# A hybrid decoder layer on one core: the first gated head's products stand two products further behind its loads, and the fourth raw block of the values is loaded later

## The chip, the core and the metric

The kernel runs on one core of one Trainium2 chip. The core has TensorE for matrix products (PE; its weight loads are listed apart as PEld), VectorE (DVE), ScalarE (ACT), GpSimd (POOL) and SyncE (SP), whose queue issues most of the transfers between the chip's memory and the core. Each engine runs its own instructions in order; semaphores order them among each other. The metric is the device time of one execution in microseconds (us). A measurement gives the median of several runs.

## The reference

One layer with 1024 tokens of width 1024, in float32. After an RMS norm, one in-projection gives nine groups of columns; eight heads of differential softmax attention and four heads of gated linear attention (GLA) work on them side by side; the out-projection joins both.

```python
h = rms_norm(x, pre_g)
z = jnp.einsum('bsd,de->bse', h, w_in)            # w_in: 1024 x 7184
qa, ka, va, ga, qb, kb, vb, gb, gk_low = split_columns(z)
oa = diff_attention(qa, ka, va, lam)              # 8 heads, values 128 wide
oa = rms_norm(oa, subln_g) * (1.0 - lam_init) * silu(ga)
log_a = log_sigmoid(gk_low @ w_gk_up + b_gk) / 16
ob = gla_chunked(qb, kb, vb, log_a)               # 4 heads, keys 128, values 256 wide
ob = rms_norm(ob, gla_g) * silu(gb)
return x + rms_norm(concatenate([oa, ob]) @ w_out, post_g)
```

(Shapes and reshapes are left out.) In `gla_chunked` a state of 128 x 256 per head is carried from chunk to chunk; within a chunk the decayed queries and keys give a masked score matrix that multiplies the values.

## The kernel before

**The in-projection** is done as products of 2 x 2 blocks with seven block products in place of eight. The columns of `w_in` are taken in 26 pairs p; the pair's weights fall into four raw blocks b11, b21 (left columns, top and bottom rows) and b12, b22 (right columns). Seven products n = 1, 2, 5, 6, 4, 7, 3 multiply one block, or one sum of blocks, with a block of the normed input. (p, n) names a product. Float32 accuracy is had by splitting each operand into a high part (ACT casts it) and a low part (DVE subtracts), so a product is three rounds of four matmuls of 128 x 512, 12 in all. Products land in accumulator banks called x (n = 1, later 6 and 7 on top), y (n = 2 or 4) and z (n = 5, later 3); `take_bank` hands out the eight banks from a list, the longest free first.

The list `order` holds the 182 products. The values of the attention heads are pairs 22 and 23 (`VALS`), done together with weights twice as wide, so that one of their products is 24 matmuls into two banks. Around them `order` runs (21,7), (22,1), (21,3), (23,1), (22,2), (23,2), (22,5), (23,5), (22,6), (23,6), (22,7) and so on through n = 4 and 3. Then pairs 24 and 25 follow.

`go(n)` emits the next n products. For each it first prepares the weights of this and the next three products (`prepare`, `make_weights`; L333 subtracts raw blocks, L352 makes high parts, L353 low parts). The weights lie in a ring of `NRING` = 5 tiles. For the values `value_weights` does this: `load_values` loads a raw block in two halves (L214), L302 subtracts blocks in place, L306 makes the two high tiles and L309 the two low ones, so that a value product's weights take four of the ring's five places. Its blocks b11 and b21 have buffers of their own. The two halves of b12 take the buffers tagged `q0` and `k0`, those of b22 `k1` and `q1`, which the gated heads use before: a load waits until the old reader is through. The third part of `go` advances a side stream, `fill`: once per product, and twice per value product.

```python
va, vb = VALS
order += [(va, 1), (va - 1, 3), (vb, 1)] + [(p, n) for n in (2, 5, 6, 7, 4, 3) for p in VALS]
...
    go(order.index((9, 3)) + 1 - made[0])
    fill.append(chain(*(gla(g) for g in range(GLA_HEADS))))
    go(len(order) - made[0] - LEAD)
```

**The gated heads** are that side stream. It begins when product (9,3) is emitted, so its first step stands behind (10,2). `gla(g)` is a generator that runs two halves of 512 tokens; between two `yield`s stand the steps of a half: the loads of keys and queries `kq` (L847, L848), values `gv` (L850) and decayed queries `gqd` (L851); the score products `pa` and the transposes `pk` (L117, L120), masked on POOL (L872), and the loads of the gates (L881); the state products `kv`; the output products `gpo` (po in the text); the squares, and the loads for the next half; the norm's product `gms`, the norm and gating on DVE (L944 to L950) and four stores to `mixe` (L952). Only the first half's loads stand directly ahead of their use; every later half's loads are issued four steps ahead. `kq` has the buffer `q0`, `gv` `k0`, `gqd` `q1`, and `k1` holds the masked scores, later the squares `sq_hl` that `gms` multiplies.

After a value product, `take_heads` adds the sums on DVE (L462), which frees the y bank, splits them (L463, L464) and stores them (L466). The weights of the out-projection are split on the side too (`wo_step`, L667 to L687, through POOL's queue).

The matmuls keep the order of the program (`keep_in_program_order`). On the other engines and on SP the order is chosen at build time by a scheduler that simulates the timeline; what stands later in the program may go earlier there.

When the 182 products end, the attention scores, values and the out-projection follow, again with an order of matmuls that is fixed at build time.

Of the kernel before, what the change touches and what calls it, by code (L numbers as in the profile page):

```python
# [31 lines left out]
def hymba_kernel(  # L32
# [23 lines left out]
    def fp(t):  # L56
        return t.bitcast(F32)
# [127 lines left out]
    def load_raw(p, halves=(0, 1)):  # L185
        if p >= len(pairs):
            return
        if p in VALS:
            return load_values("b11")
        c0 = pairs[p][2]  # L190
        for kh in halves:
            if kh not in raws.setdefault(p, {}):
                r = ap.tile([P, HB, 256], F32, tag="raw", name="w_raw", bufs=4)
                rows = slice(kh * 512, kh * 512 + 512)
                sp.dma_start(r, w_in[0, rows, c0 : c0 + 256].rearrange("(k p) c -> p k c", p=P))
                raws[p][kh] = r
# [5 lines left out]
    def load_values(name):  # L202

        if name not in value_raws:
            c0 = VA + (name[2] == "2") * 512
            r0 = (name[1] == "2") * 512
            value_raws[name] = []
            for i, tag in enumerate({"b12": ("q0", "k0"), "b22": ("k1", "q1")}.get(name, ("raw",) * 2)):
                if tag == "raw":
                    r = ap.tile([P, 2, 512], F32, tag=tag, name="v_raw", bufs=4)  # L210
                else:
                    r = kp.tile([P, 2, 512], F32, tag=tag, name="v_raw")
                rows = slice(r0 + i * 256, r0 + i * 256 + 256)
                sp.dma_start(r, w_in[0, rows, c0 : c0 + 512].rearrange("(k p) c -> p k c", p=P))  # L214
                value_raws[name].append(r)
# [74 lines left out]

    def value_weights(n):

        for name in {1: ("b11", "b21"), 2: ("b12",), 5: ("b22",), 3: ()}.get(n, ()):
            load_values(name)
        if n in (7, 4):
            load_raw(y if n == 7 else z)
        b11, b12, b21, b22 = (value_raws.get(name) for name in ("b11", "b12", "b21", "b22"))
        src = {1: b11, 2: b21, 5: b11, 6: b11, 7: b12, 4: b21, 3: b22}[n]
        sums = {5: ((b11, b12),), 6: ((b11, b22), (b21, b21)), 7: ((b12, b22),)}.get(n, ())
        for dst, a in sums:  # L300
            for i in range(2):
                dve.tensor_tensor(dst[i], a[i], (b12 if n == 7 else b11)[i], ALU.subtract)  # L302
        his, los = [], []
        for i in range(2):
            his.append(ap.tile([P, 2, 512], F32R, tag="ring", name="w", bufs=NRING))
            act.copy(his[i], src[i])  # L306
        for i in range(2):
            los.append(ap.tile([P, 2, 512], F32R, tag="ring", name="w", bufs=NRING))
            dve.tensor_tensor(los[i], src[i], fp(his[i]), ALU.subtract)  # L309
        return his, los  # L310

    def make_weights(i):
# [4 lines left out]
        if p in VALS:  # L317
            ws[i] = ws_wide[p, n] = value_weights(n)
            return
# [535 lines left out]
    def gla(g):  # L855

        u = None
        for half in range(2):
            cs = cols(half)
            kq, v, qd = gla_loads(g, half)  # L860
            gates = kp.tile([P, 2, 512], F32, tag="ks1", name="gg")
            yield
            o = kp.tile([P, 2, 512], F32, tag="ks0", name="go")
            an = kp.tile([P, 2, 4, P], F32, tag="k1", name="gan")
            a, kn = an[:, 0], an[:, 1]
# [20 lines left out]
            for m in range(2):  # L886
                kv, ib = take_bank([P, 2, 256], "kv")
                n = half * 4 + 2 * m
# [91 lines left out]
# [4 lines that stand above are left out]
    for _ in fill[0] if fill else ():  # L984
# [637 lines left out]
```

## Time and profile before

| what | value |
|---|---|
| time, median of 3 runs | 977.96 us (975.04 to 978.9) |
| the profiled execution's own time | 978.01 us |
| its span, first to last instruction | 976.3 us |
| mean granted TensorE clock | 0.997 |
| busy: PE, DVE, ACT, POOL | 953.5, 734.4, 602.5, 193.8 us |
| in-projection's products with the gated stream | about 231 to 549 us |

Times in the profile's rows count from the start of the span. A row of the timeline gives the start, the duration, the engine, the source line, the operation, what it writes and reads, how many in a row, and in brackets how long the engine had been idle before and what released it. All matmuls come from one helper line, L117, and are told apart by the names of their tiles. A matmul's duration is longer than its share of the stream, since matmuls overlap; distances between starts show the pace. A row of waits names who waited for whom, the total, the number of times and the longest. A granted clock of 1.00 is full speed.

### The profile page before, as it was taken

The numbers are of one execution on the slowest core, as the hardware profiler recorded it, in microseconds if no ns is written. First come the engines' busy times: TensorE is split into PE (matmuls) and PEld (weight loads), VectorE is DVE, ScalarE is ACT, GpSimd is POOL, SyncE is SP. The second block draws the span as 40 slices with busy tenths as digits, with TensorE's granted clock in tenths as the row PEclk, the third lists the DMA queues.
The fourth block names the chain that finished last, engine by engine and source line by source line (L and its number), as shares of the span: only waits on it lengthen the run. The fifth ranks groups of instructions, "written<-read, shape, count | busy, mean of one in ns | idle before, by whom it ended". The sixth has DMA issues, their size and how long they took to land.

```text
span 976.3 us, 15029 instructions
## 1 busy us (share of the span) xinstructions
PE 953.5 (98%) x4946; PEld 811.4 (83%) x4946; DVE 734.4 (75%) x1462; ACT 602.5 (62%) x1164; POOL 193.8 (20%) x263
## 2 busy tenths in 40 slices
PE   6999999999999999999999999999999999999997
PEld 5998988887888888888888888878888888888785
DVE  6986598896677778677675667487888888898554
ACT  8642454754677456467675444366776687887773
POOL 4300001212111111121200002121322222443322
PEclk9999999999999999999999999999999999999999
DMA  9442456578576979986763589997656669995777
GB/s 351 146 119 87 135 170 224 175 247 277 186 233 211 317 230 301 296 271 220 250 194 126 163 244 284 396 300 235 212 171 234 230 200 358 342 283 106 151 204 151
DMA packets 152301, 220.39 MB, mean 226 GB/s; under 512 B 16752, under 2 KB 87408, under 8 KB 152128
## 3 DMA queue, kind: packets, MB, share of 16 engines
q1 hardware_dynamic: 138128, 178.80, 56.9%
q0 software_dynamic: 14096, 40.64, 14.3%
q8 instruction: 39, 0.64, 0.3%
q14 instruction: 38, 0.31, 0.1%
HBM read 133.93 MB, written 88.60 MB: 228 GB/s over the span
## 4 chain that ended last, share of the span: by engine, by line
PE 86%; issue 4%; DMA 3%; DVE 3%; ACT 1%; POOL 1%; SPq 0%; DVEq 0%; POOLq 0%; ACTq 0%
PE x L117 21%; PE ypart L117 13%; PE y L117 13%; PE z L117 12%; PE sc L117 7%; PE po L117 5%; PE yps L117 4%; PE wtr L120 3%; PE gpo L117 3%; DMA wo_raw<-in_w_out_dram 1%; PE kv L117 1%; PE pa L117 1%; PE gkl_ps L117 1%; DMA kq<-gq_d 1%; DMA k_d<-qk_st 1%
## 5 line engine op out<-in xcount | busy, mean ns | idle before, releaser
L352 ACT CAST w<-w_raw 128x512 fp32r<-128x512 f32 (+1 forms) x150 | 98.1, 655 | 98.1 <-PE y L117 46.9
L353 DVE TENSOR_TENSOR w<-w_raw,w 128x512 fp32r<-128x512 f32 (+1 forms) x150 | 109.6, 733 | 45.4 <-ACT w L352 45.0
L1145 ACT ACTIVATE p<-p,stt 128x896 f32<-128x896 f32 (+7 forms) x128 | 99.3, 777 | 36.9 <-DVE stt L1135 33.8
L510 ACT COPY s<-x 128x512 f32<-128x512 f32 x72 | 42.2, 586 | 76.9 <-PE x L117 76.4
L677 POOL DMA_DIRECT2D wo_d<-wo_hi x32 | 17.7, 552 | 344.2 <-ACT wo_hi L667 344.2
L1151 POOL TENSOR_SCALAR p<-p,stt,lam 128x1024 f32<-128x1024 f32 (+3 forms) x64 | 56.2, 878 | 147.0 <-DVE stt L1150 141.4
L1135 DVE CUSTOM_DVE_ANT_0 p<-sc,maskt 128x512 f32<-128x512 f32 (+3 forms) x128 | 74.3, 585 | 14.6 <-PE sc L117 13.3
L117 PE MATMUL x<-s_hi,w 128*128 128x512 f32 x320 | 81.3, 397 | 0.0
L117 PE MATMUL z<-s_hi,w 128*128 128x512 f32 x320 | 80.1, 392 | 0.0
L117 PE MATMUL y<-h_hi,w 128*128 128x512 f32 x320 | 80.0, 392 | 0.0
L117 PE MATMUL ypart<-wo_hi,m_hi 128*128 128x512 f32 x192 | 79.5, 414 | 0.1
L117 PE MATMUL ypart<-wo_hi,m_lo 128*128 128x512 f32 x192 | 75.5, 393 | 0.0
L117 PE MATMUL ypart<-wo_lo,m_hi 128*128 128x512 f32 x192 | 75.4, 393 | 0.0
L333 DVE TENSOR_TENSOR w_raw<-w_raw 128x512 f32<-128x512 f32 (+1 forms) x88 | 65.7, 747 | 11.0 <-DMA w_raw<-in_w_in_dram 9.9
L117 PEld LDWEIGHTS x<-s_hi,w 128*128 128x128 f32 x320 | 60.7, 191 | 12.5
L117 PE MATMUL sc<-k,q 128*128 128x512 f32 (+1 forms) x192 | 69.1, 363 | 1.4 <-DVE stt L1135 1.4
L117 PEld LDWEIGHTS y<-h_hi,w 128*128 128x128 f32 x320 | 59.7, 188 | 12.2
L117 PEld LDWEIGHTS z<-s_hi,w 128*128 128x128 f32 x320 | 59.6, 188 | 12.2
L117 PE MATMUL sc<-ks,q 128*128 128x512 f32 (+1 forms) x192 | 66.2, 347 | 0.0
L1193 ACT CAST wt_hi<-wtr 128x512 fp32r<-128x512 f32 (+1 forms) x80 | 42.8, 535 | 25.6 <-PE wtr L120 24.8
L1194 DVE TENSOR_TENSOR wt_lo<-wtr,wt_hi 128x512 fp32r<-128x512 f32 (+1 forms) x80 | 50.6, 633 | 9.5 <-ACT wt_hi L1193 8.8
L1154 DVE SCALAR_TENSOR_TENSOR p<-p,stt,p 128x1024 f32<-128x1024 f32 (+3 forms) x64 | 52.1, 814 | 4.0 <-POOL p L1151 3.8
(236 smaller groups left out, 2311.2 us busy)
## 6 DMA issues: line engine op xcount, KB each, us to landing
w_raw<-in_w_in_dram SPq DMA_DIRECT2D x48, 512.0 KB, 4.7
wo_d<-wo_hi POOLq DMA_DIRECT2D x32, 256.0 KB, 2.9
q<-q_d SPq DMA_DIRECT2D x32, 256.0 KB, 4.9
k<-k_d SPq DMA_DIRECT2D x32, 256.0 KB, 5.4
ks<-k_d SPq DMA_DIRECT2D x64, 128.0 KB, 6.0
v<-v_d SPq DMA_DIRECT2D x16, 512.0 KB, 7.1
wo_raw<-in_w_out_dram POOLq DMA_DIRECT2D x31, 256.0 KB, 4.6
wo_d<-gqd POOLq DMA_DIRECT2D x22, 256.0 KB, 4.0
```

The costliest lines, as they stand in the source:

```text
L117: tc.keep_in_program_order(pe.matmul(*a, **k))
L120: tc.keep_in_program_order(pe.transpose(dst, src, ident))
L333: dve.tensor_tensor(dst, a, b, ALU.subtract)
L352: act.copy(w[0], src)
L353: dve.tensor_tensor(w[1], src, fp(w[0]), ALU.subtract)
L510: act.copy(b[k], ps)
L1135: ins = dve.tensor_tensor_reduce(p[:, a:e], sc[:, : e - a], maskt[:, NZ + P - (e - a) :] if last else maskt[:, : e - a], 1.0, 3e38 if i == ...
L1145: act.activation(p[:, :n], p[:, :n], AF.Exp, bias=st[:, m : m + 1], scale=-1.0, accum_out=st[:, 2 + m : 3 + m],)
L1151: pool.tensor_scalar(p1[:, :n], p1[:, :n], st[:, 5:6], lam, ALU.mult, ALU.mult)
L1154: dve.scalar_tensor_tensor(p0[:, :n], p0[:, :n], st[:, 4:5], p1[:, :n], ALU.mult, ALU.subtract)
L1193: act.copy(hi[:, :n], pt[:, :n])
L1194: dve.tensor_tensor(lo[:, :n], pt[:, :n], fp(hi[:, :n]), ALU.subtract)
```

## The change

Two edits. In `gla`, the first half of the first head yields twice more between its loads and its score products, so that two more products of the in-projection stand between them; every later step of the stream moves back by two turns of `go`. In `value_weights`, the load of the block b22 moves from product n = 5 to n = 6, the first that uses it.

```diff
     def value_weights(n):
-        for name in {1: ("b11", "b21"), 2: ("b12",), 5: ("b22",), 3: ()}.get(n, ()):
+        for name in {1: ("b11", "b21"), 2: ("b12",), 6: ("b22",)}.get(n, ()):
             load_values(name)
...
     def gla(g):
...
             kq, v, qd = gla_loads(g, half)
             gates = kp.tile([P, 2, 512], F32, tag="ks1", name="gg")
             yield
+            if not g and not half:
+                yield
+                yield
             o = kp.tile([P, 2, 512], F32, tag="ks0", name="go")
```

## The prediction

> **What bounds the kernel now.** I read the head of the page first, then busy time by stretches, then what TensorE waited for.
>
> ```profile
> span 976.3 us, 15029 instructions
> 0.00:241.00 241.00, 226.85 (x1329) 199.69 (x1329) 196.49 (x327) 132.47 (x222) 43.12 (x71) 1.00 0.58 191
> 241.00:616.00 375.00, 375.00 (x1815) 316.34 (x1814) 262.13 (x404) 218.79 (x382) 50.42 (x82) 1.00 0.74 238
> 616.00:930.00 314.00, 311.96 (x1633) 262.91 (x1632) 250.99 (x664) 225.90 (x486) 89.68 (x98) 1.00 0.78 244
> 930.00:976.30 46.30, 39.69 (x175) 32.48 (x174) 24.76 (x68) 25.37 (x75) 10.54 (x12) 0.97 0.75 181
> PE xT L120 <- DVE x L565: 9.0, 4, 7.5
> PE pa L117 <- DMA kq<-gq_d: 2.4, 1, 2.4
> PE sc L117 <- DVE stt L1135: 1.4, 3, 1.0
> ```
>
> In a stretch's row stand its length, then the busy time of PE, PEld, DVE, ACT and POOL, the granted clock, the DMA share and GB/s. From 241 to 616 us PE is busy 375.00 of 375.00 us, and from 616 to 930 it lacks 2.04. So almost any microsecond that the in-projection wins or loses is handed on to the end. PE's order is the program's. The one long wait outside the start-up is the one the change addresses: pa, the first product of gated head 0, waits for its loads.
>
> The place itself, PE alone, and the same product seven halves later, where its load is long there:
>
> ```profile
> 235.69 1.07 PE L117 MATMUL z<-s_lo,w 128*128 128x512 f32 x4
> 239.19 1.19 PE L117 MATMUL pa<-kq 128*128 128x128 f32 x8 [2.42 <-DMA kq<-gq_d]
> 240.88 3.31 PE L117 MATMUL x<-s_hi,w 128*128 128x512 f32 x8
> 244.94 1.98 PE L117 MATMUL y<-h_hi,w 128*128 128x512 f32 x8
> ...
> 494.78 1.98 PE L117 MATMUL z<-s_hi,w 128*128 128x512 f32 x8
> 496.60 1.07 PE L117 MATMUL z<-s_lo,w 128*128 128x512 f32 x4
> 497.50 1.05 PE L117 MATMUL pa<-kq 128*128 128x128 f32 x8
> 498.75 2.10 PE L117 MATMUL x<-s_hi,w 128*128 128x512 f32 x8
> 501.60 1.98 PE L117 MATMUL y<-h_hi,w 128*128 128x512 f32 x8
> ```
>
> From the last z group to the next product's y group takes 244.94 - 235.69 = 9.25 us at the wait and 501.60 - 496.60 = 5.00 without one: 4.25 us are lost, not 2.42. Until pa starts it is 3.50 against 0.90, so 2.60; from pa on it is 5.75 against 4.10, so 1.65 more. The clock says why:
>
> ```profile
> 236.80:239.20 2.40, 0.01 (x1) 0.04 (x1) 0.75 (x2) 1.37 (x3) 0.49 (x1) 1.00 1.04 361
> 239.20:241.00 1.80, 1.80 (x13) 1.80 (x13) 1.75 (x3) 1.50 (x3) 1.13 (x3) 0.76 1.07 414
> 241.00:242.00 1.00, 1.00 (x5) 0.81 (x4) 0.00 (x0) 0.59 (x2) 0.64 (x1) 0.50 0.92 356
> 243.00:244.00 1.00, 1.00 (x4) 0.77 (x4) 0.00 (x0) 0.00 (x0) 0.00 (x0) 0.73 0.86 262
> ```
>
> The granted clock falls to 0.50 after the gap and is back at 1.00 by 244. This wait is paid twice, and I take 4.25. The Trainium skill, "TensorE: Matmul & The Clock Gate", section "Part 1: The HAM clock gate (the "warmup" mystery)", lets the clock fall only after an idle window of about 3.4 us. By that a gap of 2.6 us would keep full speed; the trace does not agree, with 0.50 at 241 to 242 us. What the rule would make of the time here is the second rival.
>
> **The two added yields.** They put products (10,6) and (10,4), 2.72 us each (497.50 - 494.78, from the z product's first group to pa), between (10,5) and pa. Is pa then free of waiting, and are the two ready to run?
>
> ```profile
> 231.98 7.07 DMA kq<-gq_d
> 231.42 0.62 ACT L352 CAST w<-w_raw 128x512 fp32r<-128x512 f32 x1 [0.96 <-PE z L117]
> 234.12 0.62 ACT L352 CAST w<-w_raw 128x512 fp32r<-128x512 f32 x1 [2.09 <-PE y L117]
> ```
>
> The later load lands at 231.98 + 7.07 = 239.05. Without the wait (10,6) starts at 235.69 + 0.90 = 236.59 and pa 5.44 later, at 242.03: 3.0 us of margin, and nothing in the change delays that load. The weights ring has five places, so the cast that waited at 234.12 for y of (10,2) belongs to the product five further on, (11,1)'s, and the one at 231.42 is (10,7)'s; (10,6) and (10,4) had theirs before. The wait goes whole: **-4.25 us**. Should the margin fail, 4.25 is the most that stays.
>
> Every later step of the gated stream also runs two products later: in each of eight halves the gate loads (2), the next half's loads (5) and the stores to mixe (4), all on SP, one affine select on POOL, and the ACT and DVE work between. Loads, pa, kv, po and norm keep their spacing in products, PE waits for none of the later halves today, and what they read (keys, queries, values) is stored before the stream begins. I cost these moves at nothing, covered by the in-projection products between the steps; the uncovered price is the 4.25 above. No instruction is added.
>
> **The end of the stream.** The value products (22 and 23) run two stream steps each, so here the shift is not plain. Working the yields through: now po stands behind (22,1) and the norm's product gms behind (22,2); after, po stands behind (23,1) and gms behind (23,2), with (22,5) next. Three things hang on that.
>
> ```profile
> 517.34 0.90 SPq L214 DMA_DIRECT2D v_raw<-in_w_in_dram  x2
> 517.28 2.07 PE L117 MATMUL z<-s_hi,w 128*128 128x512 f32 x8
> 525.54 1.98 PE L117 MATMUL y<-w,h_hi 128*128 128x512 f32 x8
> 521.21 1.23 DVE L302 TENSOR_TENSOR v_raw<-v_raw 128x1024 f32<-128x1024 f32 x1 [7.49 <-DMA v_raw<-in_w_in_dram]
> 534.57 1.05 ACT L306 CAST w<-v_raw 128x1024 fp32r<-128x1024 f32 x1 [0.68 <-PE y L117]
> ```
>
> First, the third raw block, b12, which the diff doesn't name: its second half takes the buffer that po reads, and waits for po to end (517.28, issue 517.34, landed 521.2). Po now ends (21,3) and (23,1) later, 525.54 - 517.28 = 8.26 us, so it lands at 529.5; its subtraction is done by 530.7. The cast that needs it comes at 534.57, when a ring place is free: 3.9 us of slack. Nothing.
>
> ```profile
> 530.98 0.62 PE L117 MATMUL gms<-sq_hl,ones 128*128 128x512 f32 x2
> 531.44 2.16 PE L117 MATMUL y<-w,h_hi 128*128 128x512 f32 x8
> 535.27 1.98 PE L117 MATMUL y<-w,h_hi 128*128 128x512 f32 x8
> 537.09 1.98 PE L117 MATMUL z<-w,s_hi 128*128 128x512 f32 x8
> 547.97 1.98 PE L117 MATMUL x<-w,s_hi 128*128 128x512 f32 x8
> 531.75 0.37 SPq L214 DMA_DIRECT2D v_raw<-in_w_in_dram  x1
> 535.66 1.23 DVE L302 TENSOR_TENSOR v_raw<-v_raw 128x1024 f32<-128x1024 f32 x1 [0.17 <-DMA v_raw<-in_w_in_dram]
> 543.92 0.36 SPq L952 DMA_DIRECT2D mixe<-go  x1
> ```
>
> Second, the fourth raw block, b22: one half takes the buffer that gms reads (issued 531.75, 0.77 after gms starts, landed 3.9 later). Its first user, the weights of (22,6), must be ready at (22,6)'s start. In the new order gms starts 0.46 (531.44 - 530.98) ahead of (22,5), and (22,6) is 547.97 - 537.09 = 10.88 behind that: 11.3 us in all. Needed are 0.77 + 3.9 + 1.23 (subtraction, L302) + 1.05 (cast, L306) = 6.95. Slack 4.4. Behind the load on SP stand only stores, and behind the subtraction on DVE the low halves and the norm's tail. Nothing, while SP issues it when gms ends.
>
> Third, the accumulator banks. While both value halves hold their x sums, four banks circulate. Today's takes are y y, gms, y y, z z, so (23,2)'s second sum takes the bank of (22,2)'s first, which DVE must have read: a wait of 5.65 (537.09 - 531.44) less two products of 2.72, 0.21 us. After, the takes are y y, y y, gms, z z: that 0.21 goes, and (22,5)'s second sum takes the bank of (23,2)'s first.
>
> ```profile
> 540.28 1.28 DVE L462 TENSOR_TENSOR c<-y,s 128x512 f32<-128x512 f32 x2
> 537.40 1.22 DVE L309 TENSOR_TENSOR w<-v_raw,w 128x1024 fp32r<-128x1024 f32 x1
> ```
>
> That matmul, with all of PE's order behind it, would start 0.46 (gms) + 0.23 (one matmul: 537.09 - 535.27 is eight) = 0.69 behind (23,2)'s end. DVE has two low halves (L309, 1.22 each) to make from about 1.8 before that end, when the second group of eight is through: until +0.65; then the read L462 (half of 1.28): until +1.3. A wait of about 0.65. If DVE takes the read first it is 0; if it comes as late as today's (540.28, 3.19 behind that product's end) it is 3.19 + 0.64 - 0.69 = 3.1, and with a halved clock behind it 1.65 more: 4.8. I take 0.65, as DVE loses the norm's tail from just this place.
>
> **Sum**, against the profiled execution's own 978.01 us (span 976.3, 1.7 around it; the three runs' median is 977.96): 978.01 - 4.25 - 0.21 + 0.65 = **974.2**.
>
> **Rivals.** (1) The bank wait is long: value weights are taken ahead of the read on DVE. For it: today's read came 3.19 late. Against: what delayed it was in part the norm's tail. 978.01 - 4.25 - 0.21 + 4.8 = 978.4, no change. (2) The clock's dip at 241 belongs to something else and stays: only 2.60 comes back, 978.01 - 2.60 - 0.21 + 0.65 = 975.9. Against: the clock is 1.00 right up to the gap, falls directly behind it, and the stretches up to 930 us average 1.00. The Trainium skill's idle window of about 3.4 us ("TensorE: Matmul & The Clock Gate", section "Part 1: The HAM clock gate (the "warmup" mystery)") would have it so. (3) Slower: the later load of b22 is put behind the norm's four stores on SP, which wait for DVE. The last of them today is issued at 543.92, 12.94 behind gms. Then the weights of (22,6) are ready at 12.94 + 0.36 + 3.9 + 1.23 + 1.05 = 19.5 instead of by 11.3: a wait of 8.2, and 1.65 for the clock, 974.2 + 9.8 = 984.0. It costs from the point at which the load is issued over 5.2 us behind gms. Against: SP today issues it ahead of those stores. (4) That the change doesn't do what it says (pa still waits) has little for it with 3.0 us of margin, and is counted with (1), as it ends at no change.
>
> **How the numbers follow.** Forecast 0.70, its own range 972.5 to 976.5; rival 1 with 4, 0.12; rival 2, 0.05; rival 3, 0.13. What a measurement here can tell from no change is about 0.5%, 4.9 us: below 973.07 is faster, over 982.85 slower. The forecast is 1.1 us from the first bound, the runs before differ by 975.04 to 978.9, and with no new bank wait it is 973.5; of its 0.70 I give 0.25 to faster. Rivals 1 and 2 are the same, rival 3 is slower: 0.25, 0.62, 0.13. Range 972.0 to 981.0, leaving out the bottom of the forecast and most of rival 3, whose milder forms begin below 981.
>
> **What would show it.** Right: no wait at the first pa, three unbroken products ahead of it, granted clock 1.00 there, the whole stream to the values some 4.3 us earlier; a wait of under 1 us at the z of (22,5) for L462; none at the x of (22,6). Wrong: pa still waiting for kq, a clock dip elsewhere, PE waiting for weights from v_raw at (22,6), or L462 over 2 us behind its product. A PE gap in a stretch where there is none now would say that the shifted ACT and DVE work of the other halves isn't covered.

## The result and the profile after

Over 19 runs of each, the median is 975.10 us after the change (974.23 to 975.85) and 977.66 before (975.04 to 981.25): a ratio of 0.9977, 95% interval 0.9968 to 0.9986. The medians lie 2.6 us apart, and the ratio, which is not the quotient of the medians, gives 2.2 us. The interval leaves out 1, and the gain is under the 0.5% that the prediction called faster. The spread of the runs went from 6.2 us to 1.6.

The page's head, the middle stretch of the busy times and PE's waits of the changed kernel, in the columns of before (its profiled execution took 975.12 us):

```profile
span 973.4 us, 15020 instructions
241.00:616.00 375.00, 373.87 (x1820) 315.62 (x1819) 264.11 (x407) 220.58 (x384) 62.90 (x84) 1.00 0.77 242
PE xT L120 <- DVE x L565: 9.0, 4, 7.6
PE z L117 <- DVE c L462: 1.1, 1, 1.1
```

The line of pa is gone. A new one stands in the list, the z that waits for L462, and the stretch from 241 to 616, full before, now lacks 1.13 us. PE at the first place, with one row of the clock:

```profile
236.13 1.07 PE L117 MATMUL z<-s_lo,w 128*128 128x512 f32 x4
237.04 1.98 PE L117 MATMUL x<-s_hi,w 128*128 128x512 f32 x8
242.48 1.05 PE L117 MATMUL pa<-kq 128*128 128x128 f32 x8
243.72 2.10 PE L117 MATMUL x<-s_hi,w 128*128 128x512 f32 x8
246.57 1.98 PE L117 MATMUL x<-h_hi,w 128*128 128x512 f32 x8
...
241.00:242.00 1.00, 1.00 (x6) 0.83 (x5) 1.00 (x2) 1.00 (x3) 0.60 (x2) 1.00 1.04 410
```

The z of (10,5) is followed at 0.91 by (10,6), pa comes 5.44 later, and from pa to the product after the next it is 246.57 - 242.48 = 4.09, the undisturbed 4.10. The granted clock is 1.00. All 4.25 us came back here.

The second place, PE, DVE and SP from the start of (22,2) to the x of (22,6):

```profile
521.63 2.07 PE L117 MATMUL y<-w,h_hi 128*128 128x512 f32 x8
530.38 1.29 DVE L464 TENSOR_TENSOR c<-c,v_hi 128x512 fp32r<-128x512 f32 x2
531.59 2.35 DVE L309 TENSOR_TENSOR w<-v_raw,w 128x1024 fp32r<-128x1024 f32 x2
532.61 0.62 PE L117 MATMUL gms<-sq_hl,ones 128*128 128x512 f32 x2
533.07 0.40 PE L117 MATMUL z<-w,s_hi 128*128 128x512 f32 x1
533.30 0.37 SPq L214 DMA_DIRECT2D v_raw<-in_w_in_dram  x1
533.87 1.28 DVE L462 TENSOR_TENSOR c<-y,s 128x512 f32<-128x512 f32 x2
534.60 1.89 PE L117 MATMUL z<-w,s_hi 128*128 128x512 f32 x7 [1.14 <-DVE c L462]
545.41 1.98 PE L117 MATMUL x<-w,s_hi 128*128 128x512 f32 x8
```

One matmul of z runs, into the free bank; the second, into the bank of (23,2)'s first sum, starts at 534.60 instead of 533.30. From the first z to the x of (22,6) it is 545.41 - 533.07 = 12.34 against 10.88 before: 1.46 us given back. The load of b22 is issued at 533.30, 0.69 behind gms's start, and the x of (22,6) follows without a wait.

From the z of (10,5) to the y of (22,2) the changed kernel takes 521.63 - 236.13 = 285.50 us and the kernel before 525.54 - 235.69 = 289.85: the 4.35 us that the prediction looked for as "some 4.3". Its other sign, a wait of under 1 us at the z of (22,5), was missed: the list has 1.1, and 1.46 are lost.

In the trace's own terms: 978.01 - 4.25 - 0.21 + 1.46 = 975.01, and the profiled execution took 975.12. That it fits this closely is in part luck: the z of (10,5) comes 0.44 us later than in the profile of before (236.13 and 235.69), and the stretch from the x of (22,6) to the end is 0.3 shorter (973.4 - 545.41 = 428.0 and 976.3 - 547.97 = 428.3).

### The profile page after: what moved, and what is told of

Same layout as the page of the kernel before. It is cut to its first block, busy times and chain, and to the rows that moved or that the text cites. A ratio compares the mean times of both kernels' runs of the same rounds, so it can differ in the third digit from the quotient of the medians.

```text
span 973.4 us, 15020 instructions
## 1 busy us (share of the span) xinstructions
PE 952.3 (98%) x4946; PEld 811.1 (83%) x4946; DVE 734.2 (75%) x1462; ACT 603.0 (62%) x1164; POOL 205.7 (21%) x263
## 4 chain that ended last, share of the span: by engine, by line
PE 93%; DVE 3%; ACT 1%; DMA 1%; issue 1%; POOL 0%; DVEq 0%; SPq 0%; ACTq 0%
PE x L117 24%; PE z L117 15%; PE y L117 14%; PE ypart L117 13%; PE sc L117 7%; PE po L117 5%; PE yps L117 4%; PE wtr L120 3%; PE gpo L117 3%; PE kv L117 1%; PE gkl_ps L117 1%; PE pa L117 1%; DMA v_raw<-in_w_in_dram 1%; PE xT L120 0%; ACT junk L574 0%
```

## The experiments

Each kernel ran beside the kernel before on the same chip; that had a median of 977.15 us beside the first four below (to the filled gap) and of 977.67 beside the others. The ratios are those on record with their intervals, and not the quotients of these medians.

**Only the score products move** (an edit of the kernel before):

```diff
             yield
+            if not g and not half:
+                yield
+                yield
...
             yield
-            yield
-            yield
+            if g or half:
+                yield
+                yield
             us = [u]
```

> Edit of the kernel before: the two yields are added ahead of the first half's score products and two of the three yields behind them are taken away, so that only pa, pk and the gate loads move by two products and the rest of the gated stream, the end at the values and the load of b22 stay as they were. Theory (the wait at pa with its halved clock is worth 4.25 us, and 1.46 us of that is given back at the z of (22,5) in the changed kernel): 4.25 us under the kernel before, about 973.4 us, ratio 0.9957; no wait over 0.3 us at the first pa, clock 1.00 there, and only the old 0.2 us at the y of (23,2). Rival (pa's wait is worth only the 2.6 us that the changed kernel shows): about 975.1 us, ratio 0.9974.

Measured: 974.25 us, ratio 0.9961 (0.9946 to 0.9976). The trace has no wait at pa and none at the z:

```profile
236.55 1.07 PE L117 MATMUL z<-s_lo,w 128*128 128x512 f32 x4
242.90 1.05 PE L117 MATMUL pa<-kq 128*128 128x128 f32 x8
528.05 2.15 PE L117 MATMUL y<-w,h_hi 128*128 128x512 f32 x8
533.67 1.98 PE L117 MATMUL z<-w,s_hi 128*128 128x512 f32 x8
544.55 1.98 PE L117 MATMUL x<-w,s_hi 128*128 128x512 f32 x8
```

From z to x it is 10.88 again; the y of (23,2) keeps its wait (5.62 for 5.44). In time it lies between the two expectations, and its interval holds both; the rows decide for the theory. The first part alone gives the whole gain, and the shift of the stream's end gives some back. The profiled execution took 974.28. What keeps it from 973.4 is in part the start: PE reaches the z of (10,5) at 236.55 here and at 235.69 in the profile of before. Where that spread of the start comes from was not followed.

**The second sum of (22,5) later** (an edit of the changed kernel, in `multiply_values`):

```diff
+        terms = [
+            (j, a, b, k, u)
+            for j, (a, b) in enumerate(((0, hi), (0, lo), (1, hi)))
+            for k in range(HB) for u in range(2)
+        ]
+        if (p, n) == (VALS[0], 5):
+            terms.sort(key=lambda t: t[4])
+        for j, a, b, k, u in terms:
...
```

> Edit of the changed kernel: in product (22,5) all twelve matmuls of the first sum run ahead of the twelve of the second, so that the second sum's bank is wanted 2.7 us later. Theory (the bank wait costs 1.46 us): 1.46 us under the changed kernel and 4.4 us under the kernel before, about 973.4 us, ratio 0.9955; PE has no wait at that z. Rival (those 1.46 us only show up in another wait, the low halves of the weights or a later bank): about 975.1 us, ratio 0.9974.

Measured: 973.85 us, ratio 0.9960 (0.9945 to 0.9976). PE alone:

```profile
532.33 1.09 PE L117 MATMUL z<-w,s_hi 128*128 128x512 f32 x4
534.17 1.98 PE L117 MATMUL z<-w,s_hi 128*128 128x512 f32 x8
543.23 1.98 PE L117 MATMUL x<-w,s_hi 128*128 128x512 f32 x8
```

543.23 - 532.33 = 10.90: the wait is gone and didn't come up elsewhere before (22,6). The median is 1.25 us under the changed kernel's, though measured on other runs and with intervals that overlap. This profiled execution itself gained nothing: it took 975.20 us, the slowest of the five (the others 973.47 to 974.11) and no less than the changed kernel's 975.12. PE reached the x of (22,6) 2.18 us earlier than there and lost that again in the attention, where its list of waits has two lines that the changed kernel's lacks, and a third wait for `stt` of 0.42 us at 814.63:

```profile
PE sc L117 <- DVE wt_lo L1202: 0.5, 1, 0.5
PE sc L117 <- DMA ks<-k_d: 0.5, 1, 0.5
```

So in this execution the rival holds, at a place that it didn't name; the four faster ones have no trace. The medians of this and of the first experiment are the lowest seen, and the two can't be told apart by time.

**Only the load of b22 moves** (an edit of the kernel before; the first part of the diff alone):

> Edit of the kernel before: only the load of b22 moves from n = 5 to n = 6, no yield is added. Theory (its first half waits for gms in any case, and its second is wanted only at n = 6): ratio 1.000 within 0.001, first half still issued right behind gms. Rival (the later load comes too late, or takes DVE or SP time from something else): 1 to 5 us slower, with a wait at the x of (22,6).

Measured: 977.74 us, ratio 1.0008 (0.9995 to 1.0021): no effect, as the theory has it. SP issues the half that waits for gms 0.77 behind gms's start:

```profile
533.20 0.62 PE L117 MATMUL gms<-sq_hl,ones 128*128 128x512 f32 x2
533.97 0.37 SPq L214 DMA_DIRECT2D v_raw<-in_w_in_dram  x1
```

The move gains nothing by itself. By the code, the load's buffers would otherwise be claimed ahead of shifted steps that still use one of them (`sq_hl`), so it goes with the yields; the yields without it weren't tried.

**The gap filled** (an edit of the kernel before):

```diff
+            if not g and not half:
+                idle, ib = take_bank([P, 512], "idle")
+                for _ in range(11):
+                    mm(idle, ones, at(H["h11"][0], 0), start=True, stop=True)
+                free.insert(0, ib)
             pa, ib = take_bank([P, 4, P], "pa")
```

> Edit of the kernel before: eleven matmuls of 128 x 512 whose result nobody reads (11 x 0.227 = 2.5 us) stand ahead of the first pa, in the place of PE's idle time; pa still waits for its loads. Theory (idle PE lets the clock fall, which costs 1.65 us on top of the 2.60): clock 1.00 from 236 to 245 us and 1.65 us less, about 976.0 us, ratio 0.9983. Rival (the dip of the clock has another cause, or the clock falls for a shorter gap too): clock again 0.5 at 241 us and no gain, ratio 1.000.

Measured: 977.51 us, ratio 0.9999 (0.9989 to 1.0009). By time the rival wins, and the trace doesn't decide:

```profile
236.17 1.07 PE L117 MATMUL z<-s_lo,w 128*128 128x512 f32 x4
237.07 2.69 PE L117 MATMUL idle<-h_hi,ones 128*128 128x512 f32 x11
239.82 1.16 PE L117 MATMUL pa<-kq 128*128 128x128 f32 x8
244.03 1.98 PE L117 MATMUL y<-h_hi,w 128*128 128x512 f32 x8
...
241.00:242.00 1.00, 1.00 (x8) 0.85 (x7) 0.00 (x0) 0.99 (x2) 0.33 (x1) 1.00 1.11 408
```

The clock is 1.00, and from z to y it is 7.86 us instead of 9.25. But the loads came early in this execution: the second one of kq was issued at 232.05 and landed 6.7 us later, at 238.75. Without the eleven matmuls the gap would have been about 1.8 us, which is less than one that left the clock at 1.00 (1.96 us, below). So the trace doesn't show that filling a gap keeps the clock. It shows the price: the eleven matmuls cost their 2.5 us also where the loads come sooner, and the expectation had reckoned as if each run of the kernel before lost what its profiled one lost. That asked for its other runs. The expectation's 976.0 was missed by 1.5 us.

**The kernel before again**, two more executions with their traces:

> The kernel before, unchanged, for the spread of its runs. Theory (its runs differ because the wait at the first pa differs, by when the loads are issued, and with it the length of the halved clock): the time goes up and down with the lost time between the z of (10,5) and the y of (10,4): 978.0 us with 4.25 us lost, 975 to 976 with 1 to 2, 980 with 6. Rival (the spread comes from other places): a time that differs by over 1.5 us from this line.

> The kernel before, unchanged, a second time: the same line between the time and the loss at the first pa as in the run before this one.

Measured: 978.34 and 975.71 us. PE in the first and in the second:

```profile
235.83 1.07 PE L117 MATMUL z<-s_lo,w 128*128 128x512 f32 x4
239.50 1.13 PE L117 MATMUL pa<-kq 128*128 128x128 f32 x8 [2.60 <-DMA kq<-gq_d]
245.24 1.98 PE L117 MATMUL y<-h_hi,w 128*128 128x512 f32 x8
```

```profile
235.57 1.07 PE L117 MATMUL z<-s_lo,w 128*128 128x512 f32 x4
238.43 1.13 PE L117 MATMUL pa<-kq 128*128 128x128 f32 x8 [1.79 <-DMA kq<-gq_d]
242.59 1.98 PE L117 MATMUL y<-h_hi,w 128*128 128x512 f32 x8
```

The kernel with only b22's load moved has the same code at this place and makes a fourth case:

```profile
235.81 1.07 PE L117 MATMUL z<-s_lo,w 128*128 128x512 f32 x4
240.14 2.05 PE L117 MATMUL pa<-kq 128*128 128x128 f32 x8 [3.26 <-DMA kq<-gq_d]
247.16 1.98 PE L117 MATMUL y<-h_hi,w 128*128 128x512 f32 x8
```

The gap is pa's start less 0.90 behind the last z group; lost is z to y less the undisturbed 5.00:

| execution | gap, us | lost, us | time, us | time less lost |
|---|---|---|---|---|
| before, second of the two | 1.96 | 2.02 | 975.71 | 973.69 |
| before, profile of the prediction | 2.60 | 4.25 | 978.01 | 973.76 |
| before, first of the two | 2.77 | 4.41 | 978.34 | 973.93 |
| b22's load alone | 3.43 | 6.35 | 980.18 | 973.83 |

The last column is the same within 0.24 us while the time moves by 4.5. So these four executions differ at this one place, and as far as they show, the spread of the kernel before is the spread of this wait. The remainder is not the same for every version: the profiled executions of the score products alone and of one product (below), with nothing lost here, took 974.28 and 975.01. The median of before, 977.66, fits a loss of 3.9; its fastest run, 974.82 beside the first four kernels, one of about 1.

What moves the gap is when the load is issued, not how long it takes. SP issued the second load of kq at 231.31, 231.98, 232.45 and 232.84, in the order of the table, and pa started 7.0 to 7.3 us behind each. In the three longer gaps the profile's chain to pa goes back to a load of the out-projection's weights; in the profile of before it is

```profile
223.25 5.55 DMA wo_raw<-in_w_out_dram
```

When it has landed, ACT and DVE split it (L667, L676); behind that on DVE stand the keys (`c`, L445), and behind their store SP issues the loads. The weights landed at 228.80, 229.28 and 229.68, and the second load of kq was issued 3.2 us later each time. In the shortest gap the chain holds no such load. No run changed this order.

**One product in place of two** (an edit of the kernel before: one added yield, and b22 at n = 6):

> Edit of the kernel before: one added yield in place of two, and b22 loaded at n = 6, so that the first pa stands behind (10,6) and the stream's end moves by one turn: gms stays behind (22,2), po goes behind (21,3). Theory (what is lost at pa is the lateness of the loads, some 0 to 1 us at that place, and the end has only the old bank wait of 0.2 us at the y of (23,2)): a wait of under 1 us at pa with the clock at 1.00, no wait at the z of (22,5); 1 us under the changed kernel, about 974.2 us, ratio 0.997. Rival (a short wait drops the clock as well, or po waits for the state update that now has one product instead of two to run in): 975.5 us or more, with the clock under 1.00 at 241 us or a wait at gpo.

Measured: 974.35 us, ratio 0.9976 (0.9963 to 0.9988). In its profiled execution pa starts at 240.08, unbroken behind (10,6), and the value products have no new wait:

```profile
239.17 1.07 PE L117 MATMUL x<-s_lo,w 128*128 128x512 f32 x4
240.08 1.05 PE L117 MATMUL pa<-kq 128*128 128x128 f32 x8
```

One of its nine runs took 978.04, which none of the other versions without a gap did, and it has no trace. With the start and the loads as in the last case of the table pa would wait here again, but only from 235.81 + 0.90 + 2.72 = 239.43 to 240.14, 0.7 us; where that run lost its 3.7 us isn't known. With the first experiment it shows that the cover may be had without the shift that costs the bank wait.

**Half the gap filled** (five matmuls in place of eleven):

> Edit of the kernel before: five matmuls that nobody reads ahead of the first pa instead of eleven, so that PE idles for 1.4 us in place of 2.5 where the loads land as in the profile of before. Theory (the clock falls once PE has been idle for about two microseconds): clock stays 1.00, time like that with eleven or below, 976.3 us, as the five are less likely to outlast the wait. Rival (any gap over one microsecond drops the clock): clock 0.5 behind the gap and about 977.5 us.

Measured: 975.78 us, ratio 0.9982 (0.9971 to 0.9992).

```profile
237.06 1.31 PE L117 MATMUL idle<-h_hi,ones 128*128 128x512 f32 x5
239.46 1.13 PE L117 MATMUL pa<-kq 128*128 128x128 f32 x8 [1.09 <-DMA kq<-gq_d]
243.62 1.98 PE L117 MATMUL y<-h_hi,w 128*128 128x512 f32 x8
```

From pa to y it is 4.16, so the clock stays up behind an idle time of 239.46 - 237.06 - 5 x 0.227 = 1.27 us. That is against the rival, a drop behind any gap over 1 us. Five matmuls that nobody reads made the kernel faster by 1.8 us (0.0018 x 977.67). That they do so by keeping the clock fits, but isn't shown: without them this gap would have been 239.46 - 237.06 = 2.40 us, between 1.96, which left the clock at 1.00, and 2.60, which halved it.

## Why the prediction was right, point by point

**The wait at pa, -4.25.** It was right in mechanism and size for that execution: the wait and the halved clock went whole, and pa at 242.48 waited for nothing. The margin held, though the second load of kq was issued at 232.99, 1.0 us later than in the profile of before; it landed by 239.9, 2.6 us ahead of pa, where 3.0 had been worked out. The sum was made against one execution whose loss lay near the median, 4.25 against 3.9; had the profile caught the second execution above, the same working would have given 2.02. That the profiled one lay near the median was luck.

**The moved steps at nothing.** This was right: of the 1.13 us that PE lacks between 241 and 616 the z of (22,5) takes all, and the two kernels' lists of PE's waits agree within 0.2 us a line outside the two places.

**b12.** This was right. Its second half is issued when po ends and its subtraction waits for it; the cast stands well behind:

```profile
521.68 1.87 SPq L214 DMA_DIRECT2D v_raw<-in_w_in_dram  x2
525.90 1.23 DVE L302 TENSOR_TENSOR v_raw<-v_raw 128x1024 f32<-128x1024 f32 x1 [1.43 <-DMA v_raw<-in_w_in_dram]
530.85 1.05 ACT L306 CAST w<-v_raw 128x1024 fp32r<-128x1024 f32 x1
```

It is done at 527.1, 3.7 us ahead of the cast at 530.85; 3.9 had been worked out.

**b22.** This was right, by the issue 0.69 behind gms and by the x of (22,6), which doesn't wait. The sum of 6.95 from gms to the first cast was low: that cast (539.98, 1.05 long) ended at 541.03, 8.42 behind gms, as the subtraction ahead of it stood behind other work on DVE. The wait at the z, which delays (22,6) too, kept the slack at 4.4.

**The bank wait, +0.65.** The place, the bank and the releaser were right; this is the term of the sum that was mis-sized. It cost 1.46 us. The step that failed is "DVE has two low halves (L309, 1.22 each) to make from about 1.8 before that end". They began 1.02 before it (531.59 against 532.61), because the low parts of (22,2)'s values, L464 from 530.38, stood ahead of them on DVE. So the read behind them, L462, began 1.26 behind the product instead of 0.65. That is 0.61 of the 0.81 us that the term was short; the rest lies between the read's end and the matmul, and in the slower first matmuls behind the wait. The working had asked when the ring places come free and not what else DVE had queued at that time. The granted clock stayed at 1.00 from 532 to 538 us.

**The rivals.** (1) The long bank wait didn't come: the read began 1.26 behind its product, not 3.19. The value weights ahead of the read were in the forecast's 0.65 already; what it lacked was L464 ahead of them. (2) is out: with the gap gone the dip is gone, and without the added yields the dip came in the three traces with a gap of 2.60 us or more and not in the one with 1.96. (3) is out: SP issued the load right behind gms.

The median is 0.9 us above the forecast, of which the bank wait explains 0.81.

## What to carry to other kernels

Where a wait hangs on when a transfer is issued, its price can differ from run to run, so one profile gives one draw of it; the runs' spread is a hint, and time less the loss at that place, over several profiled runs, tells whether it explains the spread. Filler in a gap has to be weighed against the short gaps too: eleven matmuls gained nothing here. Shifting a whole stream to cover one wait also shifts how its end interleaves with the next stage: work out anew which bank and which buffer each product takes there, and count all that its releaser's engine has queued, not only the work that is named in the step. Here moving two steps and giving the turns back at once kept the end as it was.

## What the runs showed of the hardware that was not expected

A gap of PE of 1.96 us left the clock at 1.00, and those of 2.60, 2.77 and 3.43 us halved it. How long it stays halved is not in proportion to the gap. Clock rows of the first of the two executions of the kernel before, and of the kernel with b22's load alone:

```profile
240.00:241.00 1.00, 1.00 (x11) 1.00 (x9) 1.00 (x3) 0.77 (x2) 0.83 (x2) 0.89 1.07 413
244.00:245.00 1.00, 1.00 (x5) 0.85 (x4) 0.00 (x0) 0.00 (x0) 0.00 (x0) 0.90 0.94 344
```

```profile
239.00:240.00 1.00, 0.00 (x0) 0.00 (x0) 0.53 (x1) 0.97 (x2) 0.27 (x1) 0.69 1.08 399
246.00:247.00 1.00, 1.00 (x6) 0.79 (x5) 0.00 (x0) 0.00 (x0) 0.00 (x0) 0.90 0.72 242
```

Reading each edge row as part full and part half speed, the clock is halved from 240.78 to 244.20, 3.4 us, in the first, and from 239.38 to 246.20, 6.8 us, in the second: once and twice the same length. Lost less gap is 1.64 us in the first and 2.92 in the second. The rows of the prediction give 240.1 to 243.5, once more 3.4 us. Nor does the clock fall at a fixed time behind the gap's start: in the profile of the prediction and in the first of these two it fell 0.9 and 1.3 us after pa had begun, in the second 0.8 us before. The Trainium skill, "TensorE: Matmul & The Clock Gate", section "Part 1: The HAM clock gate (the "warmup" mystery)", has the clock set by a free-running window of about 3.4 us. The trace agrees with that length; it does not agree that a whole window must be idle, as gaps of 2.60 and 2.77 us sufficed. Where between 1.96 and 2.60 us the bound lies, and whether it moves with the phase of the window, stays open, as does whether matmuls put into a gap keep the clock up.
